# A hybrid encoder on one core: the gated convolution input is turned one weight piece sooner

## The chip, the cores and the metric

The kernel runs on one core of one Trainium2 chip. The metric is the device time of a run in microseconds (us). The core has a matrix engine (TensorE, PE in the profile, with its weight loads as PEld), a vector engine (VectorE, DVE), a scalar engine (ScalarE, ACT), GpSimd (POOL), and SyncE (SP), whose queue issues nearly all transfers here. The 16 DMA engines move the data. Each engine works through its own instructions in the order in which they stand, so an instruction that waits holds up all that stands behind it on that engine.

## The reference

Two layers of a mixer with three head groups over 256 tokens of width 2048, all in float32. Cut to what matters:

```python
h = rmsnorm(x, norm_g[l])
proj = h @ w_in[l]                       # 2048 x 7168, split into ten parts
a_x, a_b, a_c, a_g, d_q, d_k, d_v, d_g, m_q, m_g = jnp.split(proj, offsets, axis=-1)

u = a_c * a_x                            # group A: gated convolution, width 768
z = up[:, :-2] * w[0] + up[:, 1:-1] * w[1] + up[:, 2:] * w[2] + b
y_a = a_b * z * silu(a_g)

o_d = softmax(q1 k1) v - lam * softmax(q2 k2) v          # group D: six heads
y_d = rmsnorm(o_d) * (1 - lam_init) * silu(d_g)

y_m = softmax(m_q mk^T / sqrt(128)) mv * silu(m_g)       # group M: four heads, 256 memory tokens

x = x + concat(y_a, y_d, y_m) @ w_out[l]
```

The output is x after both layers.

## The kernel before

Every matrix product runs on PE in float32 split into two parts: a weight tile `raw` is loaded by SP, ACT casts it to its high part `hi` (L294), DVE takes the rest `lo` (L295), and PE adds three products, high by high, high by low and low by high. A weight piece is 256 rows by 512 columns (512 KB), two of the sixteen 128-row parts of the depth, and with two token tiles it gives PE 2 x 2 x 3 = 12 matmuls of 128x512. `block` (L309) goes through the eight pieces of one column block; `raw`, `hi` and `lo` have four buffers each, so a load waits until the `lo` of four pieces before is made, and a `hi` or `lo` until PE is through with the piece four before.

The column blocks of `w_in` follow one another without a pause: the D heads, the memory queries and gates, and then for the convolution B, the rest of B with a part of G, G, X, C, and the rest of X and C. Around them stands work in the background: generators in a list `tasks`, each of which does a step and says after how many weight pieces it wants the next. `run_side` (L231), which `block` calls once for each piece, advances those that are due; `later(g, n)` (L214) sets the first due time n pieces ahead. What a step writes with `keep_in_program_order` stands on its engine in this order; other instructions are placed by a scheduler when the program is built. So the due times set the order on DVE, ACT and in SP's queue.

A sheet is turned from token rows to channel rows in three moves (`turn_sheet`, L481, and `carry`, L497): DVE turns blocks of 32x32 (L485, or L704 for the memory heads), then SP writes the sheet to memory in four transfers `d<-sh` (L502), and reads it back in another order in four transfers of 128-byte runs (L506: `sh<-d`, or `bgT<-d` for the sheet below). A return waits for its write to have landed. Two sheets stand at the place in question:

- `bg` (buffer tag `bgx`, 128x1536, in the profile `sh` at L485): B times the gated G. `turn_bg` (L1191) turns it into `bgT`, which the convolution reads much later (L1216).
- The second pair of memory heads (`mem_pair`, L689): its weights `me`, 128x1024, turned at L704 into `sh`; after the return they are split on ACT and DVE (L717, L718) and multiplied on PE (L738, tile `po`).

The block X comes right behind: `ux` takes over the buffer of `bg` (L1242), and `scaled` (L1225, L1227) writes the block's two accumulators into it on ACT. It therefore waits for the four transfers that write `bg` to memory.

Of the kernel before, what the change touches and what calls it, by code (L numbers as in the profile page):

```python
# [27 lines left out]
CG = W_CONV // P  # L28
# [20 lines left out]
def encoder(ctx: ExitStack, tc: tile.TileContext, x, mem, norm_g, w_in, conv_w, conv_b,  # L49
# [21 lines left out]
    def nm(s):  # L71
        uid[0] += 1
        return f"{s}_{uid[0]}"
# [136 lines left out]
    side, tasks = deque(), []  # L210
# [3 lines left out]
    def later(g, n):  # L214
        due[id(g)] = chunk[0] + n
        return g
# [264 lines left out]
    def turn_sheet(src, dst=None, of=None, wait=5):  # L481


        if of is None:
            tc.keep_in_program_order(nc.vector.transpose(src, src))  # L485
        else:
            for t in range(NT):
                tc.keep_in_program_order(nc.vector.transpose(
                    src[:, :, :, t], of[:, t].rearrange("p (j b c) -> p b j c", b=NA, c=B)))
        if dst is None:  # L490
            dst = src.rearrange("p b j t i -> p (b j t i)").rearrange("p (j r) -> p j r", r=SEQ)
        yield wait
        yield from carry(src.rearrange("p b j t i -> p b (j t i)"),
                         dst.rearrange("p j (t a i) -> p (j t) a i", t=NT, a=NA))
        return dst
# [556 lines left out]
    for l in range(DEPTH):  # L1052
# [8 lines left out]
        def x_block(cols, order=ALLK, **how):  # L1061
            return block(xT, w_in[l], cols, order, rows=x_row_tiles, **how)
# [118 lines left out]
        def gate(g0, n, src):  # L1181

            for t in range(NT):
                a = tmp.tile([P, NB], F32, tag="nat", name=nm("a"), bufs=3)
                silu2(a[:, 0:n], src[t], st, t)
                v = by_columns(bg[:, :, g0 // P:(g0 + n) // P, t])
                nc.vector.tensor_tensor(v, v, columns(a[:, 0:n]), ALU.mult)
# [3 lines left out]
        def turn_bg(groups):  # L1191
            nonlocal bgT
            if bgT is None:
                assert all((l, d) in scored for d in range(DH))
                bgT = keep.tile([P, CG, SEQ], F32, tag="bgT", name=nm("bgT"))
            g0, g1 = groups[0], groups[-1] + 1
            yield from turn_sheet(bg[:, :, g0:g1], bgT[:, g0:g1])
            gated.update((l, g) for g in groups)
# [38 lines left out]
        gate(NB, 256, [a[:, 256:512] for a in acc])  # L1237
        acc = x_block([(C_G, NB)])
        gate(0, NB, acc)
        tasks.append(later(turn_bg(list(range(CG))), 8))  # L1240
        acc = x_block([(C_X, NB)])
        ux = sheet(keep, "bgx", CG)  # L1242
        scaled(both_rows(ux, 0, 4), acc, R2)
# [128 lines left out]
```

## Time and profile before

| | |
|---|---|
| median of 3 runs | 918.3 us (916.95 to 919.27) |
| profiled execution | 916.91 us |
| its span in the trace | 915.1 us |
| PE busy in the span | 909.1 us |
| DVE, ACT busy | 735.0 us, 509.6 us |
| mean DMA rate over the span | 235 GB/s |
| granted TensorE clock | 1.00 |

The span is the time from the first to the last instruction that the profiler recorded; the profiled execution took 1.8 us more. Times in the rows are counted from the start of the span. In a timeline a row gives start, duration, engine, line, operation, tiles, and behind it in brackets the idle time before and what ended it; SPq is SP's queue, where the duration is that of the issue and not of the transfer.

### The profile page before, as it was taken

How to read it: one execution, taken by the hardware profiler on the slowest of the kernel's cores; microseconds unless marked ns; L12 is line 12 of the kernel's file. 1: busy time of each engine (PE TensorE's matmuls, PEld its weight loads, DVE VectorE, ACT ScalarE, POOL GpSimd, SP SyncE). 2: the span in 40 equal slices, each digit the busy share in tenths (PEclk: the TensorE clock that was granted, in tenths of full speed). 3: DMA queues.
4: the chain of work that ended last, by engine and by line, in shares of the span. 5: the costliest groups of instructions: out<-in, count | busy, mean ns of one | idle time of the engine just before them, and what ended most of it. 6: DMA issues, size and time to landing. Idle time of an engine off the chain costs nothing.

```text
span 915.1 us, 12574 instructions
## 1 busy us (share of the span) xinstructions
PE 909.1 (99%) x4200; PEld 751.3 (82%) x4200; DVE 735.0 (80%) x1327; ACT 509.6 (56%) x829; POOL 38.2 (4%) x68
## 2 busy tenths in 40 slices
PE   9999999999999999999999999999999999999998
PEld 6888888888888888888888888888888888888887
DVE  5579978978789879587689878887889779498786
ACT  6667644646545556455556556586545546456352
POOL 2434010000000000000000000000000000000000
PEclk9999999999999999999999999999999999999999
DMA  8889878886787998989777882988869998988842
GB/s 297 285 247 258 284 240 226 229 264 185 197 225 187 279 252 250 237 265 244 250 221 226 266 289 74 278 210 242 246 198 207 289 243 254 242 257 238 279 155 93
DMA packets 243794, 215.18 MB, mean 235 GB/s; under 512 B 131976, under 2 KB 171720, under 8 KB 243728
## 3 DMA queue, kind: packets, MB, share of 16 engines
q1 hardware_dynamic: 238752, 208.71, 78.8%
q0 software_dynamic: 3776, 4.59, 2.0%
q10 hardware_dynamic: 1200, 1.07, 0.3%
q8 instruction: 33, 0.54, 0.2%
q14 instruction: 33, 0.27, 0.1%
HBM read 193.30 MB, written 21.00 MB: 234 GB/s over the span
## 4 chain that ended last, share of the span: by engine, by line
PE 97%; ACT 1%; DMA 1%; DVE 0%; SPq 0%; issue 0%; ACTq 0%
PE acc L305 89%; PE x L351 2%; PE acc L351 2%; PE po L523 1%; PE s L613 1%; DMA raw<-in_w_mem_kv_dram 1%; PE po L738 1%; ACT sh L450 0%; PE pt L752 0%; ACT hi L377 0%; PE s L672 0%; PE s L671 0%; PE s L670 0%; SPq L885 0%; DVE wide L380 0%; SPq L822 0%
## 5 line engine op out<-in xcount | busy, mean ns | idle before, releaser
L305 PE MATMUL acc<-hi,xT 128*128 128x512 f32 x1744 | 545.3, 390 | 0.0
L294 ACT CAST hi<-raw 128x1024 fp32r<-128x1024 f32 x264 | 275.6, 1050 | 258.4 <-PE acc L305 163.4
L295 DVE TENSOR_TENSOR lo<-raw,hi 128x1024 fp32r<-128x1024 f32 x264 | 320.6, 1219 | 107.3 <-ACT hi L294 105.6
L305 PEld LDWEIGHTS acc<-hi,xT 128*128 128x128 f32 x1744 | 327.1, 188 | 68.1
L305 PE MATMUL acc<-lo,xT 128*128 128x512 f32 x872 | 340.1, 390 | 0.0
L305 PEld LDWEIGHTS acc<-lo,xT 128*128 128x128 f32 x872 | 163.7, 188 | 33.1 <-DVE lo L295 0.3
L305 PE MATMUL acc<-hi,yT 128*128 128x512 f32 (+1 forms) x432 | 134.2, 388 | 0.0
L305 PEld LDWEIGHTS acc<-hi,yT 128*128 128x128 f32 x432 | 81.0, 188 | 16.7
L305 PE MATMUL acc<-lo,yT 128*128 128x512 f32 x216 | 83.7, 388 | 0.0
L305 PE MATMUL acc<-hi,memT 128*128 128x512 f32 x248 | 78.1, 393 | 0.0
L305 PEld LDWEIGHTS acc<-hi,memT 128*128 128x128 f32 x248 | 46.1, 188 | 9.5
L905 DVE SCALAR_TENSOR_TENSOR lo<-raw,cva,hi 128x1024 fp32r<-128x1024 f32 (+1 forms) x34 | 41.2, 1219 | 15.8 <-ACT hi L904 15.6
L305 PE MATMUL acc<-lo,memT 128*128 128x512 f32 x124 | 48.0, 391 | 0.7 <-DVE lo L905 0.7
L305 PEld LDWEIGHTS acc<-lo,yT 128*128 128x128 f32 x216 | 40.6, 188 | 8.4
L904 ACT ACTIVATE hi<-raw,cva 128x1024 fp32r<-128x1024 f32 (+1 forms) x34 | 36.7, 1100 | 13.1 <-DMA raw<-in_w_mem_kv_dram 9.5
L377 ACT CAST hi<-wide 128x1024 fp32r<-128x1024 f32 x24 | 25.0, 1059 | 28.8 <-DVE wide L380 15.5
L377 DVE TENSOR_TENSOR lo<-wide,hi 128x1024 fp32r<-128x1024 f32 x24 | 29.1, 1221 | 5.8 <-ACT hi L377 5.5
L305 PEld LDWEIGHTS acc<-lo,memT 128*128 128x128 f32 x124 | 23.3, 188 | 6.3 <-DVE lo L905 1.5
L627 ACT ACTIVATE e<-e,mx 128x256 f32<-128x256 f32 x48 | 23.8, 497 | 4.0 <-DVE mx L623 4.0
L769 POOL DMA_DIRECT2D xt<-in_x_dram x32 | 21.4, 676 | 19.4 <-DVE rsy L189 13.6
L485 DVE STREAM_TRANSPOSE sh<-sh 128x1024 f32<-128x1024 f32 (+2 forms) x14 | 17.3, 1238 | 3.1 <-ACT sh L450 3.1
L351 PE MATMUL x<-hi,sums 128*128 128x512 f32 x48 | 17.5, 392 | 0.0
(219 smaller groups left out, 779.3 us busy)
## 6 DMA issues: line engine op xcount, KB each, us to landing
raw<-in_w_in_dram SPq DMA_DIRECT2D x186, 512.0 KB, 4.7
raw<-in_w_out_dram SPq DMA_DIRECT2D x54, 512.0 KB, 4.7
raw<-in_w_in_dram SPq DMA_DIRECT2D x64, 256.0 KB, 4.3
raw<-in_w_mem_kv_dram SPq DMA_DIRECT2D x30, 512.0 KB, 6.1
d<-sh SPq DMA_DIRECT2D x88, 128.0 KB, 4.2
sh<-d SPq DMA_DIRECT2D x72, 128.0 KB, 4.2
wide<-in_w_out_dram SPq DMA_DIRECT2D x10, 512.0 KB, 6.2
wide<-in_w_in_dram SPq DMA_DIRECT2D x6, 512.0 KB, 5.7
```

Source lines behind the costliest of these rows:

```text
L294: nc.scalar.copy(hi, raw)
L295: nc.vector.tensor_tensor(lo_, raw, hi.bitcast(F32), ALU.subtract)
L305: i = nc.tensor.matmul(acc, left, right, start=start, stop=stop)
L351: nc.tensor.matmul(acc, left[a], right[b], start=first and i == 0, stop=last and i == 2)
L377: return ((hi, pin(nc.scalar.copy(hi, src))), (lo, pin(nc.vector.tensor_tensor(lo, src, hi.bitcast(F32), ALU.subtract))))
L485: tc.keep_in_program_order(nc.vector.transpose(src, src))
L523: nc.tensor.matmul(po[:, t, :], eT[:, i, t, k, :], v[:, k, h * P:(h + 1) * P], start=k == 0, stop=k == NT - 1)
L613: pin(nc.tensor.matmul(s[c][:, i, :], yT[rows, a, h, i * P:(i + 1) * P], yT[rows, b, CG + h, :], start=n == 0, stop=n == 2))
L627: nc.scalar.activation(e[:, c, i], e[:, c, i], AF.Exp, bias=mx[:, c, i:i + 1], accum_out=sm[:, c, i:i + 1])
L769: tc.keep_in_program_order(nc.gpsimd.dma_start(st[:, n], src[n * B:(n + 1) * B].rearrange("p (b r) -> b p r", b=NA)))
L904: both = (nc.scalar.activation(hi[:, j], raw[:, j], AF.Copy, scale=g), nc.vector.scalar_tensor_tensor(lo[:, j], raw[:, j], g, hi[:, j].bit ...
L905: nc.vector.scalar_tensor_tensor(lo[:, j], raw[:, j], g, hi[:, j].bitcast(F32), ALU.mult, ALU.subtract))
```

## The change

One number: the first due time of `turn_bg` is seven weight pieces ahead and no longer eight, in both layers.

```diff
         gate(0, NB, acc)
-        tasks.append(later(turn_bg(list(range(CG))), 8))
+        tasks.append(later(turn_bg(list(range(CG))), 7))
         acc = x_block([(C_X, NB)])
         ux = sheet(keep, "bgx", CG)
         scaled(both_rows(ux, 0, 4), acc, R2)
```

It adds and removes no work; it moves instructions. In SP's queue in layer 0, at the end of block X and in block C (`sh_3563` is the memory heads' second pair, `sh_2695` is `bg`; the names `raw` are the weight pieces), there stood before:

```order
L291 DMA raw_3721<-in_w_in_dram 128x2x512
L502 DMA d_3716<-sh_3563 32x4x256 x4
L291 DMA raw_3739<-in_w_in_dram 128x2x512
L506 DMA sh_3563<-d_3716 128x8x32 x4
L291 DMA raw_3761<-in_w_in_dram 128x2x512
L502 DMA d_3779<-sh_2695 32x4x384 x4
L291 DMA raw_3790<-in_w_in_dram 128x2x512
L291 DMA raw_3810<-in_w_in_dram 128x2x512
L506 DMA bgT_3663<-d_3779 128x12x32 x4
L291 DMA raw_3840<-in_w_in_dram 128x2x512
```

and in the same place of SP's queue now:

```order
L291 DMA raw_3721<-in_w_in_dram 128x2x512
L291 DMA raw_3739<-in_w_in_dram 128x2x512
L502 DMA d_3757<-sh_2695 32x4x384 x4
L291 DMA raw_3766<-in_w_in_dram 128x2x512
L502 DMA d_3716<-sh_3563 32x4x256 x4
L291 DMA raw_3790<-in_w_in_dram 128x2x512
L506 DMA bgT_3635<-d_3757 128x12x32 x4
L506 DMA sh_3563<-d_3716 128x8x32 x4
L291 DMA raw_3814<-in_w_in_dram 128x2x512
L291 DMA raw_3840<-in_w_in_dram 128x2x512
```

The writes of `bg` now stand ahead of those of the memory pair, and the two returns, eight transfers, stand together ahead of the weight piece `raw_3814` (before, `raw_3810`), which stood ahead of the return of `bg`. Layer 1 has the same new order.

On ACT in layer 0, from the cast of block C's third piece on (L1227 is `scaled` into `ux`), there stood before:

```order
L294 CAST hi_3723<-raw_3721 128x1024
L294 CAST hi_3741<-raw_3739 128x1024
L1227 ACTIVATE sh_3671<-acc_3476,st_1038 128x4x4x32
L1227 ACTIVATE sh_3671<-acc_3477,st_1038 128x4x4x32
L294 CAST hi_3763<-raw_3761 128x1024
L717 CAST v_3519<-sh_3563 128x512
L294 CAST hi_3792<-raw_3790 128x1024
L717 CAST v_3519<-sh_3563 128x512
L294 CAST hi_3812<-raw_3810 128x1024
```

(rows of L261, L264 and L724 between them are left out), and now, with the same left out:

```order
L294 CAST hi_3723<-raw_3721 128x1024
L1227 ACTIVATE sh_3671<-acc_3476,st_1038 128x4x4x32
L1227 ACTIVATE sh_3671<-acc_3477,st_1038 128x4x4x32
L294 CAST hi_3741<-raw_3739 128x1024
L294 CAST hi_3768<-raw_3766 128x1024
L294 CAST hi_3792<-raw_3790 128x1024
L717 CAST v_3519<-sh_3563 128x512 x2
L294 CAST hi_3816<-raw_3814 128x1024
```

`scaled` stands one cast earlier, and the cast of the sixth piece stands ahead of both splits of the memory pair's sheet, where it stood between them.

On DVE in layer 0, where the two sheets are turned (L485 turns `bg`, L704 the second head of the pair), there stood before:

```order
L295 TENSOR_TENSOR lo_3620<-raw_3617,hi_3619 128x1024
L684 TENSOR_SCALAR me_3417<-me_3417,mr_3420 128x256 x2
L704 STREAM_TRANSPOSE sh_3563<-me_3417 128x4x128
L295 TENSOR_TENSOR lo_3648<-raw_3645,hi_3647 128x1024
L485 STREAM_TRANSPOSE sh_2695<-sh_2695 128x1536
L295 TENSOR_TENSOR lo_3679<-raw_3676,hi_3678 128x1024
L295 TENSOR_TENSOR lo_3701<-raw_3698,hi_3700 128x1024
```

and now, with the short rows between them left out in both:

```order
L295 TENSOR_TENSOR lo_3620<-raw_3617,hi_3619 128x1024
L485 STREAM_TRANSPOSE sh_2695<-sh_2695 128x1536
L295 TENSOR_TENSOR lo_3650<-raw_3647,hi_3649 128x1024
L684 TENSOR_SCALAR me_3417<-me_3417,mr_3420 128x256 x2
L295 TENSOR_TENSOR lo_3679<-raw_3676,hi_3678 128x1024
L704 STREAM_TRANSPOSE sh_3563<-me_3417 128x4x128
L295 TENSOR_TENSOR lo_3701<-raw_3698,hi_3700 128x1024
```

`bg` is turned one piece sooner, and the memory head two pieces later; up to `lo_3701` the same work is done in another order. PE's instructions stand as before.

## The prediction

> **What bounds the kernel now.** I read the head of the page first, for the time that PE leaves free.
>
> ```profile
> span 915.1 us, 12574 instructions
> PE 909.1 (99%) x4200; PEld 751.3 (82%) x4200; DVE 735.0 (80%) x1327; ACT 509.6 (56%) x829; POOL 38.2 (4%) x68
> ...
> PE 97%; ACT 1%; DMA 1%; DVE 0%; SPq 0%; issue 0%; ACTq 0%
> ```
>
> PE is idle for 915.1 - 909.1 = 6.0 us, and the chain that ends last lies on PE for 97% of the span. A change that adds no work and leaves PE's order alone can win only what PE waits for where the change acts. So the next view is that of the waits on PE alone:
>
> ```profile
> PE warm L128 <- DVE zeros L123: 1.2, 1, 1.2
> PE acc L305 <- DVE lo L905: 0.7, 2, 0.5
> PE acc L922 <- ACT hi L904: 0.3, 1, 0.3
> ```
>
> All three are the start of the program and the memory's weights (L905, L904); none is in the block that the change touches. The windows of block C in layer 0 and of its end in layer 1 say the same:
>
> ```profile
> 375.00:385.00 10.00, 10.00 (x45) 8.26 (x44) 3.75 (x6) 4.98 (x9) 0.00 (x0) 1.00 1.01 267
> 792.00:802.00 10.00, 10.00 (x49) 8.38 (x48) 5.34 (x6) 3.98 (x5) 0.00 (x0) 1.00 1.03 279
> ```
>
> PE is busy for 10.00 of 10.00 us at a granted clock of 1.00, and the DMA share is 1.01 and 1.03: beside PE the DMA engines are full there. Then the waits of all engines, for what the change aims at, and the timelines of ACT and DVE beside it:
>
> ```profile
> ACT sh L1227 <- DMA d<-sh: 10.2, 2, 5.3
> ```
>
> ```profile
> 373.69 1.05 ACT L294 CAST hi<-raw 128x1024 fp32r<-128x1024 f32 x1 [1.52 <-issue]
> 380.02 1.27 ACT L1227 ACTIVATE sh<-acc,st 128x512 f32<-128x512 f32 x2 [5.28 <-DMA d<-sh]
> 381.17 1.05 ACT L294 CAST hi<-raw 128x1024 fp32r<-128x1024 f32 x1
> ...
> 389.40 1.05 ACT L294 CAST hi<-raw 128x1024 fp32r<-128x1024 f32 x1 [3.63 <-DMA raw<-in_w_in_dram]
> ```
>
> ```profile
> 365.13 1.77 DVE L485 STREAM_TRANSPOSE sh<-sh 128x1536 f32<-128x1536 f32 x1
> ...
> 369.03 1.23 DVE L295 TENSOR_TENSOR lo<-raw,hi 128x1024 fp32r<-128x1024 f32 x1
> ...
> 382.25 1.22 DVE L295 TENSOR_TENSOR lo<-raw,hi 128x1024 fp32r<-128x1024 f32 x1 [6.25 <-ACT hi L294]
> ```
>
> In each layer `scaled` (L1227) waits some 5 us for `bg` to be written, the next cast stands behind it, and DVE's next `lo` comes 6.25 us late, done at 382.25 + 1.22 = 383.47. Whether PE feels that is told by the chain:
>
> ```profile
> 370.85 21.80 PE acc L305 x96
> ...
> 778.42 21.80 PE acc L305 x96
> ```
>
> 96 matmuls are eight pieces of 12, so a piece takes 21.80 / 8 = 2.725 us, a matmul 0.227. The first of the eight is X's last, and C's nth piece begins at 370.85 + n x 2.725. C's fifth piece, the late one, begins at 384.48 and needs its `lo` one matmul later, at 384.7. It came at 383.47: 1.2 us to spare. The wait that the change removes eats nearly all of the lead, but costs PE nothing.
>
> **What the change moves, and its price.** SP's queue before, in layer 0 and then the rows of layer 1 that differ in length:
>
> ```profile
> 364.13 2.25 SPq L502 DMA_DIRECT2D d<-sh  x4
> 366.48 0.39 SPq L291 DMA_DIRECT2D raw<-in_w_in_dram  x1
> 368.74 2.93 SPq L506 DMA_DIRECT2D sh<-d  x4
> ...
> 372.39 2.57 SPq L502 DMA_DIRECT2D d<-sh  x4
> 375.06 1.51 SPq L291 DMA_DIRECT2D raw<-in_w_in_dram  x2
> 377.86 6.42 SPq L506 DMA_DIRECT2D bgT<-d  x4
> 384.33 15.45 SPq L291 DMA_DIRECT2D raw<-in_w_in_dram  x17
> ```
>
> ```profile
> 778.43 4.55 SPq L506 DMA_DIRECT2D sh<-d  x4
> ...
> 785.99 5.56 SPq L506 DMA_DIRECT2D bgT<-d  x3
> ...
> 793.04 0.75 SPq L506 DMA_DIRECT2D bgT<-d  x1
> ```
>
> First, `bg` is turned one piece sooner on DVE (1.77 us ahead of one `lo`). DVE was done with that `lo` some 5 us before PE's need (PE begins X's last piece at 370.85, and the `lo` after it is done by 366), so this costs nothing; its cover is that lead.
>
> Second, the writes of `bg` are issued when the turn, one more `lo` and a load are done. The turn ended at 365.13 + 1.77 = 366.90 with that `lo` ahead of it; now the memory head's rows are no longer ahead, and I take 366, where the issue was at 372.39. With the slowest landing of the four before,
>
> ```profile
> L502 SPq DMA_DIRECT2D d<-sh x4: 432/467/1076, 372.4 to 373.9; - x4
> ...
> DMA to landing us min/median/max: 5.3/5.7/6.0
> ```
>
> they have landed at about 373, while X's accumulators are complete at 370.85 + 2.73 = 373.58. So `scaled` starts at about 373.8, and both waits, 10.2 us of ACT's idle time, go. Worth on PE: 0, by the chain. The cast that now stands behind `scaled` is that of C's fourth piece: 373.8 + 1.27 + 1.05, and 1.22 for `lo`, is 377.3, against PE's need at 381.75 + 0.23. The fifth piece follows at about 379.7, with 5 us to spare where it had 1.2.
>
> Third, the returns. What is late next is the seventh piece of C (`raw_3814`), behind eight return transfers instead of ahead of four. SP reaches them once `lo_3701` is made and its load issued; that is the DVE row at 369.03 (done at 370.26, as DVE's work up to it is the same), so at about 371, and the first return of `bg` can go when its write has landed, 366 + 5.3 = 371.4. From there I bound the piece by the issue rows above and these of the transfers around it (the rates are in 40 slices of 360 to 392):
>
> ```profile
> GB/s 129 193 366 133 238 392 383 373 325 211 229 325 165 176 111 172 128 89 259 373 396 398 312 308 362 345 239 165 135 54 114 192 137 210 294 342 387 370 361 353
> ...
> raw<-in_w_in_dram SPq DMA_DIRECT2D x7, 512.0 KB, 5.0
> ...
> sh<-d SPq DMA_DIRECT2D x4, 128.0 KB, 3.4
> ```
>
> Slow: 6.42 for the return of `bg`, 4.55 for that of the pair (layer 1's), 5.0 from the load's issue to its landing: 371.4 + 15.97 = 387.4, and 2.3 for cast and `lo` (1.05 and 1.22): 389.7. PE begins the piece at 370.85 + 7 x 2.725 = 389.93 and needs `lo` at 390.15: 0.45 us to spare. Fast, with 2.93 for the pair's return: 388.1, 2.05 to spare. The two splits of the pair's sheet on ACT, which stand ahead of that cast, need its return landed: in the slow case 382.4 + 3.4 = 385.8, and two casts of at most 0.65 end at 387.1, before the load lands. In layer 1 the rows are
>
> ```profile
> 771.81 1.77 DVE L485 STREAM_TRANSPOSE sh<-sh 128x1536 f32<-128x1536 f32 x1
> ...
> 776.30 1.23 DVE L295 TENSOR_TENSOR lo<-raw,hi 128x1024 fp32r<-128x1024 f32 x1
> ```
>
> ```profile
> L506 SPq DMA_DIRECT2D bgT<-d x4: 440/1226/3280, 786.0 to 793.0; - x4
> ...
> DMA to landing us min/median/max: 4.4/6.9/7.2
> ```
>
> ```profile
> 796.84 1.05 ACT L294 CAST hi<-raw 128x1024 fp32r<-128x1024 f32 x1 [3.80 <-DMA raw<-in_w_in_dram]
> ```
>
> The turn with the `lo` ahead of it ended at 773.6, so the writes go at about 773.4 and the first return at 778.7, behind the load that the `lo` at 776.30 frees. 5.56 + 0.75 = 6.31, then 4.55 or 2.93, 5.0 and 2.3 give 796.9 or 795.2, against 778.42 + 19.08 + 0.23 = 797.73: 0.85 to 2.5 to spare.
>
> The pair's products on PE (`po`, at 392.65) stand a piece behind that and need the splits done by 388.5 or so: covered. `bgT` is read only in the output stage, and no other queue is passed, since POOL and ACT issue no transfer here.
>
> A harder bound: by the order before, the load issued at 384.33 landed just ahead of its cast at 389.40, at 389.3, with the same bytes ahead of it and the seventh piece besides. If the DMA engines are no better fed than they were, the seventh piece lands one piece earlier, 389.3 - 1.4 = 387.9 (524 KB at the rate of the slices of 392, 383 and 373 GB/s), and its `lo` is made at 390.2, 0.1 us late. In layer 1 the last return, issued at 793.04, landed 4.4 later, at 797.4, behind the load cast at 796.84; less a piece 796.0, so `lo` at 798.3, 0.6 us late. Together +0.7, the upper end of this term. Against it, SP stood still before while writes landed, and now issues other writes in that time. I take 0, since both sums from the issue rows leave time to spare; the lower end is 0 too, as PE has no idle time there to give back.
>
> The Trainium skill would price the eight returns lower: "DMA: Bandwidth & Descriptors", sections "Why small descriptors are slow (HBM only)" and "Where 436 GB/s comes from", gives a fixed cost of about 3 bus cycles a packet. By its 32 bytes a cycle a 128-byte packet takes 7 cycles, at its 850 MHz 8.2 ns; the 10,240 packets over 16 engines would be an estimate of 5.3 us where the issue rows sum to 9.35 or 10.97. By that the piece would come 4 us sooner and the sum still be 0; the rows decide, since SP's issue is what holds the load back.
>
> Sum: 0 (turn) + 0 (the wait on ACT) + 0 (returns, 0 to +0.7). The profiled execution took 916.91 us with a span of 915.1; it stands 1.4 below the median of 918.3, so against the median the forecast is **918.3 us**.
>
> **The rivals.** *Slower: the returns hold back the seventh piece.* The place is SP's queue ahead of `raw_3814`; it decides once that piece lands later than 387.8 in layer 0 or 795.4 in layer 1, and from there each microsecond is one on PE. For it: the DMA engines are full, and one transfer of a return has held SP for up to 3.28 us (the row of `bgT` above) where another took 0.75. Against it: both sums end in time. By the harder bound it gives 918.3 + 0.7 = 919.0. With one more transfer in each layer at the slow pace of some 2.6, 1.9 more than 0.75, on top of the slow sums, it is (1.9 - 0.45) + (1.9 - 0.85) = 2.5: 920.8.
>
> *Faster: the thin piece was late in other runs.* The runs spread from 916.95 to 919.27, and C's fifth piece has 1.2 us to spare; if what lifts the median over the profiled execution is PE waiting for it, the change gives that back, 918.3 - 916.9 = 1.4 us: 916.9. For it: the lead is thin in both layers. Against it: PE does not wait there in this trace, and nothing in it tells that the slower runs lost their time at this place.
>
> *The change does not do what it says:* `bg` lands so late that `scaled` still waits. The fourth piece has 4 us of cover, and the time is 918.3 all the same.
>
> **The numbers.** A measurement of this kernel can tell about 0.3% (2.75 us) from no change. The forecast has 0.65 and the last rival 0.05; the thin piece 0.14, of which 0.04 beyond 0.3% if runs lose more there than the median shows; late returns 0.16, of which 0.10 beyond 0.3%, as margins under 1 us are no more than one slow transfer. So faster 0.04, same 0.70 + 0.10 + 0.06 = 0.86, slower 0.10. The range reaches from the thin piece's 916.9, less 0.9 for the spread of a median, to the late returns' 920.8 and a little over: 916.0 to 921.0.
>
> **What would show it.** Right: no row of ACT's L1227 waiting for `d<-sh`; the fifth piece's `lo` 5 us ahead of PE; PE busy 10.00 in both windows; the seventh piece's `lo` made before 390.15 and 797.7; PE's busy time at 909 us and the chain still 97% on PE. Wrong: a wait of PE at L305 for DVE's L295 or ACT's L294 at about 390 or 797, or for L718 ahead of L738. The prediction fails if the returns, standing together, take SP over 12 us, or if PE waits somewhere outside these blocks in a way that this trace does not show.

## The result and the profile after

The changed kernel took 921.29 us (median of 20 runs, 918.43 to 924.94) beside 919.42 us for the kernel before (20 runs, 916.95 to 921.82): a ratio of 1.0023 with a 95% interval of 1.0013 to 1.0034. That is 1.2 to 3.1 us slower, a loss smaller than the 0.3% that I had set as the least a measurement can tell, yet the interval lies clear of no change. The forecast was no change.

The profiled execution of the changed kernel took 923.46 us, 2.2 above the median, where that of the kernel before, 916.91, lay 2.5 below its own; so the two profiles differ by more than the medians do. The head of its page and its chain:

```profile
span 921.7 us, 12571 instructions
PE 911.9 (99%) x4200; PEld 752.9 (82%) x4200; DVE 735.6 (80%) x1327; ACT 510.9 (55%) x829; POOL 38.1 (4%) x68
...
PE 86%; DMA 4%; SPq 3%; DVE 3%; ACT 2%; issue 1%; ACTq 0%; DVEq 0%
```

PE is still 99% busy, but the chain lies on it for 86% and no longer 97%; SP's queue and the transfers have come in. The waits on PE say what for (us in total, times, longest):

```profile
PE acc L305 <- DVE lo L295: 3.9, 4, 2.4
```

This row is new: four waits for a `lo`. Two are in layer 1's D heads, of which more below; the other two are the seventh pieces of block C, one in each layer. This is the chain there, first in layer 0 and then in layer 1 (start, duration, what):

```profile
384.61 0.68 SPq L506
385.39 4.55 DMA raw<-in_w_in_dram
390.05 1.06 ACT hi L294
391.13 1.24 DVE lo L295
392.41 2.83 PE acc L305 x11
...
797.19 4.35 DMA raw<-in_w_in_dram
801.64 1.06 ACT hi L294
802.72 1.24 DVE lo L295
804.00 2.79 PE acc L305 x11
```

PE gave out its first matmul of the piece at 391.39 and at 803.07, and the second, which needs `lo`, 1.01 and 0.94 us later instead of 0.23: it lost 0.79 + 0.71 = 1.50 us. The matmuls right behind each wait start a little further apart than 0.227 us, which costs 0.13 us more each time: against the kernel before, PE is 0.92 and 0.84 us later at the end of these pieces. Right behind the last return (the row of L506) the load is issued, and after it nothing is waited for but the load's own landing, its cast and its `lo`. SP's timeline shows how late it came to that load:

```profile
367.54 2.61 SPq L502 DMA_DIRECT2D d<-sh  x4
370.25 0.77 SPq L291 DMA_DIRECT2D raw<-in_w_in_dram  x1
371.12 2.73 SPq L502 DMA_DIRECT2D d<-sh  x4
373.95 0.40 SPq L291 DMA_DIRECT2D raw<-in_w_in_dram  x1
374.44 6.95 SPq L506 DMA_DIRECT2D bgT<-d  x4
381.50 3.79 SPq L506 DMA_DIRECT2D sh<-d  x4
385.39 13.90 SPq L291 DMA_DIRECT2D raw<-in_w_in_dram  x16
...
785.43 6.59 SPq L506 DMA_DIRECT2D bgT<-d  x4
792.14 4.96 SPq L506 DMA_DIRECT2D sh<-d  x4
797.19 14.09 SPq L291 DMA_DIRECT2D raw<-in_w_in_dram  x16
```

SP stands idle nowhere from 367.5 on: the two writes, the loads and the eight returns follow one another with some 0.1 us between the rows. On ACT the change did what it says:

```profile
374.67 1.29 ACT L1227 ACTIVATE sh<-acc,st 128x512 f32<-128x512 f32 x2 [0.88 <-PE acc L305]
...
388.30 1.14 ACT L717 CAST v<-sh 128x512 fp32r<-128x512 f32 x2 [6.49 <-DMA sh<-d]
390.05 1.05 ACT L294 CAST hi<-raw 128x1024 fp32r<-128x1024 f32 x1 [0.60 <-DMA raw<-in_w_in_dram]
```

`scaled` waits for the accumulators alone, 0.88 us. In its place ACT now waits 6.49 us for the memory pair's return at L717, and then for the seventh piece. The 5.3 us moved from one row of ACT to another.

Of the 6.6 us between the two profiled spans (921.7 and 915.1), 1.63 are in the first 80 us of the program, 1.76 at the two seventh pieces, and about 3.2 at two pieces of layer 1's D heads (near 615 and 637 us). Nothing in the order of any engine differs there between the kernels, and whether the change has a part in it is taken up with the last runs.

### The profile page after: what moved, and what is told of

Its sections match the earlier page's. It is cut to its first block, busy times and chain, and to the rows that moved or that the text cites. A ratio compares the mean times of both kernels' runs of the same rounds, so it can differ in the third digit from the quotient of the medians.

```text
span 921.7 us, 12571 instructions
## 1 busy us (share of the span) xinstructions
PE 911.9 (99%) x4200; PEld 752.9 (82%) x4200; DVE 735.6 (80%) x1327; ACT 510.9 (55%) x829; POOL 38.1 (4%) x68
## 4 chain that ended last, share of the span: by engine, by line
PE 86%; DMA 4%; SPq 3%; DVE 3%; ACT 2%; issue 1%; ACTq 0%; DVEq 0%
PE acc L305 79%; SPq L506 3%; PE x L351 2%; DMA raw<-in_w_in_dram 2%; PE acc L351 2%; DVE lo L295 1%; DMA d<-sh 1%; PE po L523 1%; PE s L613 1%; ACT hi L294 1%; PE acc L922 1%; ACT sh L450 1%; PE po L738 0%; DMA raw<-in_w_mem_kv_dram 0%; PE pt L752 0%
## 5 line engine op out<-in xcount | busy, mean ns | idle before, releaser
L305 PE MATMUL acc<-hi,xT 128*128 128x512 f32 x1744 | 545.5, 390 | 0.0
L295 DVE TENSOR_TENSOR lo<-raw,hi 128x1024 fp32r<-128x1024 f32 x264 | 320.9, 1220 | 101.3 <-ACT hi L294 99.6
L305 PEld LDWEIGHTS acc<-hi,xT 128*128 128x128 f32 x1744 | 327.1, 188 | 68.0
L305 PE MATMUL acc<-lo,xT 128*128 128x512 f32 x872 | 340.5, 390 | 3.9 <-DVE lo L295 3.9
L305 PEld LDWEIGHTS acc<-lo,xT 128*128 128x128 f32 x872 | 163.7, 188 | 38.3 <-DVE lo L295 5.6
L305 PE MATMUL acc<-hi,yT 128*128 128x512 f32 (+1 forms) x432 | 134.2, 388 | 0.0
L305 PEld LDWEIGHTS acc<-hi,yT 128*128 128x128 f32 x432 | 81.0, 188 | 16.7
L305 PE MATMUL acc<-lo,yT 128*128 128x512 f32 x216 | 83.7, 388 | 0.0
L305 PE MATMUL acc<-hi,memT 128*128 128x512 f32 x248 | 78.0, 392 | 0.0
L305 PEld LDWEIGHTS acc<-hi,memT 128*128 128x128 f32 x248 | 46.2, 188 | 9.3
L305 PE MATMUL acc<-lo,memT 128*128 128x512 f32 x124 | 47.9, 390 | 0.0
L305 PEld LDWEIGHTS acc<-lo,yT 128*128 128x128 f32 x216 | 40.6, 188 | 8.4
L305 PEld LDWEIGHTS acc<-lo,memT 128*128 128x128 f32 x124 | 23.3, 188 | 5.2 <-DVE lo L905 0.4
L485 DVE STREAM_TRANSPOSE sh<-sh 128x1024 f32<-128x1024 f32 (+2 forms) x14 | 17.3, 1238 | 3.1 <-ACT sh L450 3.1
```

Of the source, the lines that this page charges most:

```text
L295: nc.vector.tensor_tensor(lo_, raw, hi.bitcast(F32), ALU.subtract)
L305: i = nc.tensor.matmul(acc, left, right, start=start, stop=stop)
```

## The experiments

The theory (A): the seventh piece's load comes too late because SP works off eight returns ahead of it. The rivals: chance waits of one execution (B); something that turning `bg` sooner costs by itself (C); the DMA engines, whichever queue issues the returns (D); ACT's conversion of the pair at L717, which stands ahead of the cast (E). The table has what TensorE lost at the seventh piece of C in the profiled execution, worked out from the starts of the matmuls at the beginning of the piece (what lies between one and the next beyond the usual 0.23 us), and the ratio to the kernel before with its interval.

| run | lost at the seventh piece, layer 0 / 1, us | ratio |
|---|---|---|
| changed kernel | 0.79 / 0.71 | 1.0023 (1.0013 to 1.0034) |
| the same again | 0.75 / 0 | 1.0013 (1.0002 to 1.0024) |
| the same, third profile | 0.26 / 0 | |
| sooner in layer 0 alone | 0.18 / 0 | 1.0003 (0.9992 to 1.0014) |
| sooner in layer 1 alone | 0 / 1.27 | 1.0003 (0.9994 to 1.0012) |
| `bg`'s return one piece later | 0 / 0 | 1.0008 (0.9995 to 1.0021) |
| `bg`'s return on GpSimd's queue | 0 / 0 | 0.9998 (0.9986 to 1.0010) |
| all returns on GpSimd's queue | 0 / 0 | 1.0003 (0.9994 to 1.0012) |
| due six pieces ahead | 0 / 0 | 1.0002 (0.9990 to 1.0014) |
| due four pieces ahead | 1.33 / 0.34 | 1.0006 (0.9997 to 1.0014) |
| returns in the other order | 0 / 0 | 0.9997 (0.9989 to 1.0006) |
| the returns apart | 0 / 0 | 1.0006 (0.9996 to 1.0015) |
| kernel before, profiled again | 0 / 0 | |

**One layer alone.** The due time stays eight in the other layer:

```diff
-        tasks.append(later(turn_bg(list(range(CG))), 7))
+        tasks.append(later(turn_bg(list(range(CG))), 7 if l == 0 else 8))
```

> Theory A (the seventh weight piece of stage C is issued by SP behind eight return transfers, and TensorE waits for it once in each layer, 0.79 us in layer 0 and 0.71 us in layer 1): with the piece sooner in layer 0 alone, the wait of TensorE stands at the seventh piece of layer 0 (0.6 to 0.9 us beyond the 0.23 us pitch) and none stands at the seventh piece of layer 1, whose load is issued behind four returns; the time is about 0.8 us over the kernel before (ratio 1.0009), half of what the change lost. Theory B (the loss lies elsewhere, in chance stalls that differ between executions): the wait at the seventh piece comes and goes, and the time is anywhere between the two kernels whichever layer is changed. Theory C (turning sooner costs VectorE's and ScalarE's order something in each layer): also half the loss, but without a wait at the seventh piece.

and its mirror, `8 if l == 0 else 7`:

> The piece sooner in layer 1 alone. Theory A: a wait of TensorE at the seventh piece of layer 1 (0.3 to 1 us) and none at that of layer 0, where four returns stand ahead of it as before; ratio 1.0004 to 1.0015. Theory B: no tie between the layer that is changed and where TensorE waits.

Each time TensorE waits in the changed layer and not in the other. The sizes were off: 0.18 us in layer 0 where 0.6 to 0.9 was expected, 1.27 in layer 1. The ratios are 1.0003 both, below what A gave for either, and their intervals hold the 1.0009 as well as no change at all. So the place is settled by this pair, the price is not.

**The changed kernel again.**

> The changed kernel once more, beside new runs of the kernel before. Theory A (SP is held by the eight returns ahead of the seventh piece's load): TensorE waits for VectorE at the seventh piece in both layers again (each 0.3 to 1.1 us beyond the pitch), and the ratio is 1.001 to 1.003. Theory B (chance stalls of the one profiled execution): the wait at the seventh piece is not there, or the ratio is that of no change (1.000, within 0.0010).

The wait in layer 0 is there (0.75), but in layer 1, where A had one too, the piece came in time with 0.19 us to spare. The loss repeats on another set of runs, at 1.0002 to 1.0024, so it is no chance of the first set. The wait itself is at an edge: a few tenths of a microsecond in SP's queue decide whether it shows.

**The return one piece later.** The turn and the writes stay where the change put them; only the return waits three pieces and not two behind its write.

```diff
-        yield 2
+        yield gap          # 3 for bg, 2 for the others
         of = d.rearrange("b c a (n i) -> (b c) a n i", i=B)
```

> The turn and the writes of bg as in the changed kernel, but its return to on-chip memory comes one weight piece later, behind the pair's return and the seventh piece's load. Theory A: SP issues the seventh piece's load behind four returns only, the wait of TensorE at the seventh piece goes in both layers (under 0.1 us beyond the pitch), ScalarE's wait for bg's writes stays away, and the time is that of the kernel before within 0.5 us (ratio 0.9995 to 1.0005). Theory C (turning and writing sooner is itself what costs): the time stays at about 1.002 of the kernel before, and the time is lost somewhere else than at the seventh piece. A gain below the kernel before would need that ScalarE's old wait of 5 us for bg's writes had cost TensorE something in the ordinary run.

SP's order here:

```profile
376.28 3.25 SPq L506 DMA_DIRECT2D sh<-d  x4
379.57 0.58 SPq L291 DMA_DIRECT2D raw<-in_w_in_dram  x1
380.20 5.74 SPq L506 DMA_DIRECT2D bgT<-d  x4
```

The seventh load goes at 379.57, behind four returns, and its `lo` is 4.5 us ahead of PE; the wait is gone in both layers, and no other of over 0.1 us has come in block C. ACT's old wait for the writes stays away too. Theory C falls for the place: turning and writing sooner costs nothing at the seventh piece. The ratio, 0.9995 to 1.0021, is too wide to say by itself that the loss is gone.

**The return on another queue.**

```diff
-            tc.keep_in_program_order(nc.sync.dma_start(to[:, :, a], of[:, a]))
+            tc.keep_in_program_order(back.dma_start(to[:, :, a], of[:, a]))   # nc.gpsimd for bg
```

> The turn and the writes of bg as in the changed kernel, its four return transfers at the same place, but issued by GpSimd's queue: the same bytes in the same runs move at the same time, SP is not held by them. Theory A (SP is held while it issues the returns): SP comes to the seventh piece's load some 6 us sooner, the wait at the seventh piece goes, and the time is that of the kernel before within 0.5 us. Theory D (it is the DMA engines that are busy with the returns, whoever issues them): the seventh piece's load is issued sooner but lands no sooner, its landing takes 7 us and more instead of 4.6, TensorE waits there as in the changed kernel (0.5 to 0.9 us a layer), and the time stays at 1.001 to 1.002.

The wait goes, and the ratio is that of no change, as A has it. But the reason was only half A's. GpSimd's and SP's timelines:

```profile
374.07 4.06 POOL L506 DMA_DIRECT2D bgT<-d  x4 [247.61 <-DVE sh L741]
```

```profile
374.33 1.01 SPq L291 DMA_DIRECT2D raw<-in_w_in_dram  x2
378.29 9.26 SPq L506 DMA_DIRECT2D sh<-d  x4
387.59 3.83 SPq L291 DMA_DIRECT2D raw<-in_w_in_dram  x7
```

Without `bg`'s return on its queue, SP was held by the pair's four transfers for 9.26 us, where in the changed kernel they took 3.79. With four of the eight on another queue, SP's time for returns fell only from 10.74 us to 9.26 (from 11.55 to 9.32 in layer 1): the four that stayed on SP took longer while those of GpSimd were under way, as theory D has it. (How much of that is GpSimd's doing is not shown apart: standing first behind two loads, the pair's return took SP 6.51 us in a run below without any return on another queue.) Theory D is right about the landing as well: the seventh load, issued at 374.84, took 12.4 us to land (11.3 in layer 1), where it took 4.6 and 4.4 in the changed kernel. But it still landed 4.8 us ahead of TensorE's first matmul of the piece, and not 1.4. What saved the seventh piece is that its load stood ahead of the hold (the second of the two loads at 374.33). The eighth piece, behind it, came 1.1 us ahead of TensorE in layer 0. The Trainium skill ("DMA: Bandwidth & Descriptors", section "Issuing engines are not separate DMA queues") says that transfers from all engines run on the same 16 DMA engines and that another issuer saves only the issuer's own time; these rows agree with the first, and put the second at 1.5 us of SP's time (2.2 in layer 1), not at the 6.95 that `bg`'s return had taken there.

**All returns on GpSimd's queue.** The same edit for every turned sheet.

> The changed kernel with all returns of turned sheets (bg's, the pair's and those of the other stages) issued by GpSimd's queue, so that SP is never held by a return. Theory A: no wait of TensorE at the seventh piece, and the eighth piece, which was the thinnest with bg's return alone on GpSimd (1.1 us ahead in layer 0), comes 2 us and more ahead too; the time is that of the kernel before or up to 1 us less (ratio 0.999 to 1.0005), since TensorE is then short of a weight piece nowhere in stage C. Theory D (the DMA engines, not the issuing queue, are what the returns fill): the pieces of stage C land as late as in the changed kernel, and the ratio is 1.001 to 1.002.

The seventh and the eighth piece came 3.3 and 5.6 us ahead in layer 0 (2.9 and 5.1 in layer 1), as expected, and the ratio is 1.0003: with leads to spare everywhere in C, nothing is won against the kernel before. TensorE had no idle time there to give back. The rows of SP's loads at 380 to 384 us, issued while GpSimd's returns were under way, show that full DMA engines alone do not hold a queue (least, median and longest, in ns for the issue and in us for the landing):

```profile
L291 SPq DMA_DIRECT2D raw<-in_w_in_dram x4: 367/415/722, 380.1 to 383.3; - x4
...
DMA to landing us min/median/max: 6.5/9.3/9.8
```

At a DMA share of 0.99 (380 to 385 us) four loads took SP 0.37 to 0.72 us each to issue, but 6.5 to 9.8 us to land. In all profiles together no weight load took SP over 2.4 us to issue, nor a write over 1.9, where a return took up to 6.0.

**One more piece sooner.**

```diff
-        tasks.append(later(turn_bg(list(range(CG))), 7))
+        tasks.append(later(turn_bg(list(range(CG))), 6))
```

> The turn of bg one further piece sooner, so that the writes and the returns of bg and of the pair stand apart on SP: a return of bg lies between the loads of the fifth and the sixth piece, and the seventh piece's load is ahead of the pair's return. Theory A (only what stands ahead of the seventh piece's load counts): no wait of TensorE at the seventh piece; a smaller one may come at the fifth or the sixth piece, whose loads now stand behind bg's return and the pair's writes; the time is that of the kernel before within 0.7 us (ratio 0.9995 to 1.0008). Theory C (the sooner bg is turned the more is lost): a ratio above that of the changed kernel, 1.003 and more.

No wait in C, the seventh piece 3.1 and 2.9 us ahead, and 1.0002: the order of places 8, 7, 6 is not an order of times. Theory C is out.

**Three more pieces sooner** (4 for 7 in the same line).

> The turn of bg three further pieces sooner: bg's writes and returns stand whole pieces ahead of the pair's writes, so the two sets of returns lie apart on SP, with loads of weight pieces between them. Theory A: the seventh piece's load stands behind at most four returns, and no wait of TensorE comes there; the time is that of the kernel before within 0.7 us (ratio 0.9992 to 1.0008). Theory C (the sooner bg is turned the more is lost): 1.003 and more.

The ratio is as expected, but the wait is not gone: 1.33 us in layer 0, the longest there of all runs, and 0.34 in layer 1, although SP issued the seventh load ahead of the pair's return. SP's and ACT's timelines in layer 0:

```profile
366.84 6.72 SPq L506 DMA_DIRECT2D bgT<-d  x4
373.61 1.62 SPq L291 DMA_DIRECT2D raw<-in_w_in_dram  x2
375.33 3.21 SPq L502 DMA_DIRECT2D d<-sh  x4
378.63 0.92 SPq L291 DMA_DIRECT2D raw<-in_w_in_dram  x2
382.23 4.23 SPq L506 DMA_DIRECT2D sh<-d  x4
```

```profile
389.11 1.14 ACT L717 CAST v<-sh 128x512 fp32r<-128x512 f32 x2 [3.49 <-DMA sh<-d]
390.16 1.99 ACT L294 CAST hi<-raw 128x1024 fp32r<-128x1024 f32 x2
```

The load (the second of the two at 378.63) landed at 386.13. Its cast stands behind L717 on ACT, and L717 waited for the pair's return, which landed at 389.01. Here theory E holds: `bg`'s return had held SP for 6.72 us ahead of the pair's writes, so the pair's return was late, and the piece paid through ACT's order. The number of returns ahead of the load is not the whole story; whatever ACT has ahead of the cast counts as well.

**Load or conversion, in the changed kernel itself.** To tell A from E there, two edits: the pair's return asked for one piece later, which turns the two returns round, and the pair's conversion two pieces later, which lets the scheduler put the seventh load between the two returns. (In these two runs the pair's products, L738, also stand one and two pieces later on PE.)

```diff
-        yield from carry(sh..., eT...)
+        yield from carry(sh..., eT..., 3)      # returns in the other order
...
-        yield 1
+        yield 3                                # the returns apart: ahead of L717
         for k in range(NT):
```

> The returns of the memory heads' pairs are asked for one piece later, so that in layer 0 the pair's four returns stand ahead of bg's four (in layer 1 one of bg's, then the pair's, then three of bg's); the seventh piece's load still stands behind all eight. ScalarE's conversion of the pair, which has one of its two halves ahead of the seventh piece's cast, gets its data some 7 us sooner in layer 0. Theory A (the seventh load, held behind eight returns): the wait of TensorE at the seventh piece stays, 0.3 to 1.1 us in layer 0, and the weight's landing is what ends last ahead of ScalarE's cast. Theory E (ScalarE's conversion, waiting for the pair's return ahead of the cast, is what makes the seventh piece late): no wait there in layer 0, and one of under 0.5 us in layer 1. Time by theory A 1.0005 to 1.002, by theory E 0.9995 to 1.0005.

No wait came in either layer, by 0.43 us in layer 0 and 0.47 in layer 1, though the load stood behind all eight returns. That is E's number and not A's; but the rows don't bear E's reason out:

```profile
372.03 6.51 SPq L506 DMA_DIRECT2D sh<-d  x4
378.58 4.38 SPq L506 DMA_DIRECT2D bgT<-d  x4
383.06 17.07 SPq L291 DMA_DIRECT2D raw<-in_w_in_dram  x18
```

```profile
387.97 1.05 ACT L294 CAST hi<-raw 128x1024 fp32r<-128x1024 f32 x1 [5.94 <-PE acc L305]
```

ACT was idle for 5.94 us with the first half of L717 done, and the cast began 0.1 us after the load had landed (387.87; the row names PE, which was done long before). So the load decides here and not the conversion. It was in time because SP came to the returns sooner: against PE's first matmul of the piece (390.48 here) the load was issued 7.42 us ahead, in the changed kernel 6.00 and 5.88. From the first return to the load's issue it took 11.03 us, as in the changed kernel (10.95), but SP came to the first return 18.45 us ahead of that matmul, where it was 16.95. Both sets of writes had gone out in one go, ahead of both loads. What counts is when SP reaches the returns, plus about 11 us, not their order. In the changed kernel the load decided too, but only just: L717 ended at 389.44 and the load landed at 389.95, so a sooner load alone would have won 0.5 of the 0.79 us.

> The conversions of the pair stand two pieces later in the program's list, and with them SP's order becomes: bg's four returns, the seventh piece's load, the pair's four returns, the eighth piece's load; the cast of the seventh piece stands ahead of the pair's conversion on ScalarE. The mirror of the run in which bg's return went behind: bg's return stays where the change put it. Theory A: the seventh load is issued some 4 us sooner, no wait of TensorE at the seventh piece; the eighth, behind the pair's conversion, comes 0 to 2 us ahead; ratio 0.9995 to 1.0008. A wait at the seventh piece of over 0.3 us in both layers would speak against it.

The seventh piece came 2.1 and 3.8 us ahead, as expected. The eighth, whose load now stands behind the pair's return, was late by 0.66 us in layer 0 and 0.13 in layer 1, where 0 to 2 us to spare was expected: the bill goes to the next piece in the queue.

**The waits in the D heads.** In the profile of the changed kernel PE lost some 2.7 us at a piece near 637 us in layer 1, and in its second profile 0.76 (the wait and the slower matmuls behind it). Both kernels were profiled once more.

> The kernel before, profiled once more. The order of all instructions at layer 1's D heads (about 634 to 637 us) is the same in both kernels, and TensorE waited there 2.56 us in the first profile of the changed kernel and 0.63 us in the second, not in the one profile of before. If that wait belongs to both kernels, it shows here too or is a matter of chance between executions (0 to 2.6 us); no wait at the seventh pieces of stage C in either layer, and 1 to 3 us between the fifth piece's low part and TensorE's need.

> The changed kernel, profiled a third time, beside the last run on the same chip. Theory A: a wait at the seventh piece of at least one layer, 0.2 to 1.3 us, and the seventh piece's low part under 0.5 us ahead in the other; no wait at L1227 for the writes.

The kernel before lost 0.69 us there this time (0.19 in its first profile), the changed kernel 3.75 (1.6 of them at a slower clock, shown at the end), in executions of 917.74 and 920.99 us, beside 917.23 for another of the kernel before; among the other runs it was 0.5 for due four, 1.2 for due six and 1.9 for the returns in the other order. So the wait belongs to both kernels. That it was longest in two of the three profiles of the changed kernel is not explained: nothing is reordered there, and five profiles don't tell chance from cause. What kind of wait it is, the traces do tell. SP issues four returns there; ACT (L552) and DVE (L553, L623, L621) work on what they bring, and the piece's `lo` stands behind that on DVE. These are the returns in the first profile of the kernel before, and then of the changed kernel:

```profile
620.22 5.01 SPq L506 DMA_DIRECT2D sh<-d  x4
```

```profile
625.26 5.67 SPq L506 DMA_DIRECT2D sh<-d  x4
```

In the kernel before, the `lo` was made 0.01 us ahead of PE's need, so this place has no margin in either kernel. SP was through with the four returns 8.2 and 7.7 us ahead of the piece's first matmul in the two profiles of the kernel before, and 5.7, 7.8 and 6.3 us in the three of the changed kernel; PE's wait alone was 0.04 and 0.55, and 2.56, 0.63 and 2.04 us. The wait goes roughly with that, so it is SP's returns here too; why SP was later with them is what stays open. At the seventh piece, the third profile lost 0.26 us in layer 0 and nothing in layer 1 (0.19 to spare).

## Why the prediction was wrong

*What bounds the kernel.* Right. In every profile the time is PE's, and what a version lost in block C is what PE waited.

*The turn on DVE, at nothing, and the wait on ACT, at nothing.* Right, both. L1227 no longer waits for `d<-sh`; the fifth piece's `lo` is 5.83 us ahead (1.1 before), the fourth's 5.3. And none of it was worth anything, as the runs that keep these leads and have no wait at the seventh piece show (1.0002 due six pieces ahead, 1.0003 with all returns on GpSimd's queue).

*The third term, the returns, taken as 0.* This is the step that failed. "SP reaches them once `lo_3701` is made and its load issued … so at about 371, and the first return of `bg` can go when its write has landed, 366 + 5.3 = 371.4." The writes did go at 366 and land when I said (starts of layer 0 less the 1.63 us by which this execution is shifted: issued at 365.9, the first landed at 371.5). But SP was not free: ahead of the returns it also had to issue a load, the pair's four writes and the sixth load, and came to them at 372.8, 1.4 us later; in layer 1 1.0 later. From the quoted rows that could have been summed: 366 + 2.57 for `bg`'s writes + 0.39 for a load + 2.25 for the pair's writes + 0.75 for a load is 371.96, and with the slow sum behind it the `lo` is made at 390.23, 0.1 us late instead of 0.45 early. Measured, it was 6.90 us from `bg`'s first write to the first return (6.94 in layer 1) where these rows give 5.96: the pair's writes took 2.73 for 2.25, the first load 0.77 for 0.39, and some 0.1 us lie between the rows. I waited for data where SP's own work was what took longest. The rest of the sum:

| | layer 0, forecast | measured | layer 1, forecast | measured |
|---|---|---|---|---|
| SP reaches the returns | 371.4 | 372.8 | 778.7 | 779.7 |
| the eight returns, to the load's issue | 10.97 | 10.95 | 10.86 | 11.76 |
| load, issue to landing | 5.0 | 4.55 | 5.0 | 4.35 |
| `lo` ahead of PE's need | +0.45 | -0.73 | +0.85 | -0.65 |

(Measured starts are less 1.63 and 5.73 us, the shift of this execution.) The slow holds that I took as an end were the normal case; the landing was a little better. Some 0.26 us more come from two small slips in each layer: cast and `lo` took 2.40 us from the landing and not 2.3, and PE begins the piece 0.16 us sooner than the sum had it (in the kernel before at 389.77 and not at 389.93), so that the true margins of the slow sums were 0.3 and 0.7 us.

*The harder bound*, which I wrote down and set aside, came nearest: with the DMA engines no better fed, the load lands at 387.9 and 796.0 for +0.7 in all. It landed at 388.3 and 795.8, for 1.50. The windows of the changed kernel show the premise, DMA engines full (share 1.06) at 199 GB/s where the same window held 267 before; and PE's loss is just behind the windows that I had named:

```profile
375.00:385.00 10.00, 10.00 (x46) 8.28 (x45) 4.34 (x5) 4.61 (x7) 0.00 (x0) 1.00 1.06 199
386.00:393.00 7.00, 6.38 (x29) 4.96 (x28) 2.98 (x4) 3.29 (x5) 0.00 (x0) 1.00 1.13 313
```

The estimate from the packet cost in the Trainium skill ("DMA: Bandwidth & Descriptors", section "Why small descriptors are slow (HBM only)"), 5.3 us for the eight returns, is off by a factor of two here: they took 10.95 and 11.76. Other transfers shared the DMA engines with them (the sixth load, issued ahead of them, landed 5.5 us after the first return was issued), which the estimate leaves out.

*The rivals.* The slower one named the place, the queue and the row in which it shows, and its price of 0.7 to 2.5 us holds the 1.50 of the profile and most of the measured interval. I gave it 0.16 against 0.65, by margins of 0.45 and 0.85 us that were smaller than the error of the sum they came from. The faster rival is out: the fifth piece's lead went up by 4.7 us and nothing was won. The third did not happen. Of the signs that I had named, the wait of PE at L305 for L295 came, while the returns did not take SP over 12 us in this execution (10.95 and 11.76).

*The size.* Of the 3.0 us between the forecast and the median of 921.29, 1.1 is the kernel before, whose three runs at 918.3 became 919.42 over twenty; the rest is the change. What the seventh pieces lost in the three profiles, 1.50, 0.75 and 0.26 us, is on average 0.8 us, or 1.0 with the slower matmuls right behind each wait; the two measured differences are 2.1 and 1.2 us. The interval of the second, 0.2 to 2.2 us, holds this, that of the first, 1.2 to 3.1, does not. So the seventh pieces may be only a part of the loss; what the rest is, and whether the waits in the D heads belong to it, is not settled.

*The versions.* All versions without a wait at the seventh piece have an interval that holds 1.000, and none is faster than the kernel before beyond its interval. The three other versions with such a wait hold 1.000 too: times alone separate only the changed kernel from the kernel before, and the place rests on the profiles.

## What to carry to other kernels

When a move puts transfers ahead of a load in a queue, sum the queue's own issues from the last point where it stood idle, and not from the event that makes the data ready; if the margin that is left is smaller than the spread of one issue, the stall belongs in the forecast. A wait taken from an engine that was not the bound wins nothing, and the transfers that made it wait must stand somewhere: look for the load or the cast that they now stand ahead of. Where returns in short runs fill the DMA engines, move the urgent load ahead of them. Another queue for half of the returns freed SP for only 1.5 to 2.2 us here; with all of them there, SP's loads were issued at once but landed after up to 9.8 us.

## What the hardware did that I had not expected

One transfer in 128-byte runs held SP's queue for anything from 0.4 to 6.0 us, the longest in layer 1 of the run with `bg`'s return on GpSimd. This is the row for L506 in layer 0 of that run, of the pair's four transfers of 128 KB (least, median and longest, in ns):

```profile
L506 SPq DMA_DIRECT2D sh<-d x4: 366/1796/5157, 378.3 to 386.9; - x4
```

In that run the DMA engines were full (share 1.08 from 378 to 383 us) with returns of which half came from another queue. Which of the transfers the hold falls on differs between executions. The sum is steadier: from the first return's issue to the load's, 10.4 to 12.3 us in the ten places where all eight stood together on SP.

In the third profile of the changed kernel, PE's wait of 2.0 us in the D heads was followed by eight matmuls at 0.427 us instead of 0.227, 1.6 us lost beside the wait. Windows and timeline:

```profile
633.00:636.00 3.00, 1.35 (x6) 0.77 (x5) 3.00 (x4) 2.12 (x9) 0.00 (x0) 1.00 0.35 134
636.00:640.00 4.00, 3.77 (x10) 2.95 (x11) 4.00 (x7) 4.00 (x11) 0.00 (x0) 0.57 0.58 147
640.00:650.00 10.00, 10.00 (x46) 8.27 (x45) 9.00 (x15) 6.03 (x7) 0.00 (x0) 1.00 0.69 210
```

```profile
636.23 0.65 PE L305 MATMUL acc<-lo,xT 128*128 128x512 f32 x1 [1.88 <-DVE lo L295]
```

The granted clock fell to 0.57 on average over these 4 us and was back at 1.00 after. An idle time of 2.4 us at the same place in the first profile (the longest in the row of the waits on PE above) was not followed by it. The Trainium skill ("TensorE: Matmul & The Clock Gate", section "HAM oscillation — how this bites in real kernels") puts the rule at no idle gaps above some 3.4 us; here 1.9 us of idle time was followed by the lower clock once, and 2.4 was not in another execution. In this one, a wait of 2.0 us cost 3.7 with what the slower clock added.
